# A hybrid backbone layer on one core: six fill tiles of the attention move into the Strassen stage, and TensorE's order in attention is written out as a software pipeline

## The chip, the core and the metric

The kernel runs on one core of a Trainium2 chip. A core has five engines that run side by side, each through its own list of instructions: TensorE (PE in the profile; its weight loads are the row PEld), VectorE (DVE), ScalarE (ACT), GpSimd (POOL) and SyncE (SP, which here only issues DMAs). They wait for one another through semaphores. Operands lie in the on-chip memory SBUF (128 partitions); matmul results go to PSUM, eight banks of 128 x 512 fp32 values.

The metric is the device time of the program in microseconds. Before the change it is 1123.3 us, the median of three runs (1123.12 to 1123.35).

## What is computed

One layer over 1024 latent tokens (a grid of 16 rows and 64 columns) and 256 context tokens, width 1024, fp32. The input is normalised and modulated (`h`), one wide projection feeds three branches, and the branches are merged by sigmoid gates and projected once more:

```python
h, gate = modulate(x, c, norm_g, w_ada, b_ada)
z = h @ w_in                                   # 1024 x 8704
q, k, v = per-head normalised queries and keys, values
ya = neighbourhood_attention(q, k, v, kc, vc, rpb) * silu(z[..., A_Z:B_B])
yb = bg * dw_conv(cg * val, w_conv) * silu(gz)                 # 3 taps
yc = silu(layer_norm(dw_conv(a * sigmoid(g), w31) + b)) * silu(zc)
ga, gb, gc = split(sigmoid(z[..., GATES:]), 3)
m = ga * (ya @ w_out_a) + gb * (yb @ w_out_b) + gc * (yc @ w_out_c)
x = x + gate * (m @ w_o)
```

The attention has 8 heads of 64. A query sees a clamped window of 8 rows and 16 columns with a learned bias, and all 256 context keys, in one softmax.

## The kernel before

Every fp32 operand of a large matmul is split into two rounded parts, hi and lo; a product then takes three matmuls: hi x hi, hi x lo, lo x hi (`mm3`, line 103). The 8704 columns of the wide projection are cut into tiles of 128 columns. A tile computed directly takes 2 halves of the tokens x 8 steps of depth x 3 = 48 matmuls with 512 moving columns. In the Strassen stage two tiles are computed as a pair (`group`, line 787): seven products `product` (line 770) of 4 x 3 matmuls instead of eight, with sums of the weight blocks made on POOL (`s1` to `s4`), and with sums `T` of blocks of `h` that were made earlier (`h_sums`, line 645), stored, and loaded and split again by `load_t` (line 714).

The stages, in order of time in the trace:

1. The front: modulation, the normalised `h` in its two parts (`hlf`), the queries, keys and values of the first head pair, the context, the first tile pair of the gated unit (`glu(0)`).
2. Attention. `attend(hp)` (line 586) does the four head pairs; `scores` (548) and `turned` (577) are called in 32 rounds: a round is two blocks of 128 queries of one head. In a round TensorE computes context scores `sc` and local scores `sl`; DVE adds the bias and takes the minimum (line 567); ACT makes the exponentials (568, 569); DVE sums, inverts and scales (571 to 574); TensorE transposes the probabilities (581); ACT and DVE split them into `phi` and `plo` (583, 584); TensorE multiplies them with the values (`weigh`, 598) into `py`. The score banks `sc`, `sl` and `py` exist once, the transposes' bank `pp` twice. Before a head starts, `stacks` (506) makes its split operands and `bias_of` (527) its bias image.
   The softmax chain is long, so TensorE is given fill: the queries, keys and values of the next pair (`qkv`, 130), the tiles of the gated unit (`glu`, 259), four tiles of the attention's gate path (`plain(ZA + i)`, 678), four of the short convolution's gate path (`plain(BZ + i)`, 680), and, behind the last round, two tiles of merge gates (line 725). Nobody writes down where the fill goes: the program is traced stage by stage, and a planner with a model of the engines orders each engine's list.
3. The Strassen stage: 17 groups of two tiles by `run` (952), with three steps each, then `last_two` (887) for two more pairs. Beside it DVE computes the 31-tap convolution, `conv_step(4)` and `conv_step(3)` in each group (124 steps of two instructions in all).
4. The merge of the three branches and the last projection, again by Strassen.

SBUF before: `a1` and `at` hold what attention needs and are closed behind it; `tp` (line 685) with the twelve blocks `T`, 4 KB a partition each, opens only then, so the operands of the Strassen stage are loaded behind the last round, beside the two merge gate tiles.

## Time and profile before

| | |
|---|---|
| median of three runs | 1123.3 us |
| the profiled execution | 1122.98 us, of which its span from first to last instruction is 1121.2 us |
| attention with its fill, from the first scores to the last value matmuls | 125.46 to 501.40 us |
| the two merge gate tiles behind it | 501.40 to 524.53 us |
| Strassen stage | 524.53 to about 905 us |
| merge and last projection | to 1121.2 us |
| granted TensorE clock | 0.989 of full speed on average, 1.00 in attention and in the Strassen stage |

A row of the timeline has the start and the duration in us, the engine, the line of the kernel, the operation, what it writes and reads, the shapes, and how many alike were merged; in brackets, how long the engine sat idle before it and what released it. A row of a group has line, engine, operation and shapes with its count, then the busy time in us, the mean duration in ns, and the idle time before. Matmuls overlap: the next starts before the last has ended, so the cost of one in a dense list is the distance between starts, not its duration. A row of a stretch has from and to, its length, the busy time and instructions of PE, PEld, DVE, ACT and POOL, the TensorE clock, the share of the DMA engines and GB/s.

### The profile page before, as it was taken

Reading aid. Unit: us, or ns where it says so; the run is one execution under the profiler, and the core shown is the slowest. Engines: PE = TensorE matmul, PEld = TensorE weight load, DVE = VectorE, ACT = ScalarE, POOL = GpSimd, SP = SyncE. Lnnn points to the kernel's source line nnn. Section 1 sums busy time; section 2 is a strip of 40 time slices with the busy share of each in tenths; the row PEclk is TensorE's granted clock in tenths of the full one; section 3 lists DMA queues with packets and bytes.
Section 4 is the critical chain, followed back from the end, with each engine's and each line's share of the span. In section 5 each row is a group of like instructions: output and inputs, shape, how many; then the busy total and the mean of one; then the engine's idle time right before and its main releaser. Section 6 shows DMA issues by size and latency. Waiting matters only on the chain. (4 is left out here: it accounts for less than half of the span.)

```text
span 1121.2 us, 15882 instructions
## 1 busy us (share of the span) xinstructions
PE 1084.2 (97%) x5330; PEld 923.2 (82%) x5330; DVE 832.6 (74%) x1368; ACT 519.8 (46%) x1108; POOL 653.8 (58%) x643
## 2 busy tenths in 40 slices
PE   6889999999999999999999999999999999999998
PEld 5768898998998888887888888888888788878766
DVE  6983478666765655557995997897992479879995
ACT  6764576567556554445233232323434434533430
POOL 2254957437636951104958586868777562783860
PEclk7999999999999999999999999999999999999999
DMA  9555414313312332218133424343436996462443
GB/s 351 203 190 190 122 44 120 94 57 93 118 54 85 122 120 70 67 49 326 38 132 104 151 85 160 103 153 139 129 134 237 408 327 222 140 215 66 126 155 122
DMA packets 79458, 163.17 MB, mean 146 GB/s; under 512 B 10289, under 2 KB 31153, under 8 KB 79281
## 3 DMA queue, kind: packets, MB, share of 16 engines
q1 hardware_dynamic: 74768, 160.06, 41.5%
q10 hardware_dynamic: 4608, 2.10, 0.6%
q8 instruction: 42, 0.69, 0.3%
q14 instruction: 40, 0.32, 0.1%
HBM read 120.18 MB, written 44.50 MB: 147 GB/s over the span
## 5 line engine op out<-in xcount | busy, mean ns | idle before, releaser
L751 DVE SCALAR_TENSOR_TENSOR cv<-upad,cf_t,cv 128x512 f32<-128x512 f32 x240 | 166.8, 744 | 0.1
L699 POOL TENSOR_TENSOR wl<-s,wh 128x512 fp32r<-128x512 f32 x69 | 98.4, 1439 | 21.8 <-ACT wh L698 8.1
L90 POOL TENSOR_TENSOR wl<-wr,wh 128x384 fp32r<-128x384 f32 (+1 forms) x57 | 57.3, 1012 | 68.2 <-ACT wh L88 57.6
L698 ACT CAST wh<-s 128x512 fp32r<-128x512 f32 x92 | 55.9, 616 | 87.6 <-POOL s L702 66.0
L584 DVE TENSOR_TENSOR plo<-pp,phi 128x256 fp32r<-128x256 f32 (+2 forms) x96 | 54.5, 576 | 34.8 <-ACT phi L583 34.4
L541 POOL TENSOR_TENSOR bias<-mk,img 64x96 f32<-64x96 bf16 (+1 forms) x96 | 43.7, 462 | 36.9 <-DVE mn L567 20.5
L699 POOL TENSOR_TENSOR wl<-wr,wh 128x512 fp32r<-128x512 f32 x44 | 60.5, 1375 | 4.2 <-ACT wh L698 4.2
L775 PE MATMUL ga<-ha,wh 128*128 128x512 f32 x152 | 59.3, 390 | 1.2 <-ACT wh L698 1.2
L777 PE MATMUL ga<-ha,wl 128*128 128x512 f32 x152 | 59.2, 390 | 0.0
L776 PE MATMUL ga<-ha,wh 128*128 128x512 f32 x152 | 59.2, 390 | 0.0
L583 ACT CAST phi<-pp 128x256 fp32r<-128x256 f32 (+2 forms) x96 | 46.5, 494 | 26.6 <-PE pp L581 25.9
L567 DVE CUSTOM_DVE_ANT_0 pt<-sl,bias,mn 128x384 f32<-128x384 f32 (+1 forms) x64 | 37.2, 581 | 23.0 <-PE sl L564 21.7
L88 ACT CAST wh<-wr 128x384 fp32r<-128x384 f32 (+1 forms) x66 | 31.6, 487 | 39.8 <-PE zaps L108 14.3
L568 ACT ACTIVATE pt<-sc,mn 128x256 f32<-128x256 f32 x64 | 30.4, 475 | 40.1 <-DVE mn L567 40.0
L581 PE MATMUL pp<-ident,pt 128*128 128x128 f32 x304 | 47.0, 273 | 1.6 <-DVE pt L574 1.6
L803 POOL TENSOR_TENSOR s<-wr 128x512 f32<-128x512 f32 x16 | 23.8, 1486 | 38.7 <-DMA wr<-in_wz 38.6
L581 PEld LDWEIGHTS pp<-ident,pt 128*128 128x128 f32 x304 | 37.4, 140 | 9.0 <-ACT phi L583 1.3
L79 POOL TENSOR_TENSOR ssh<-ssh,half_neg 128x4 f32<-128x4 f32 (+1 forms) x40 | 41.4, 1036 | 2.9
L574 DVE TENSOR_SCALAR pt<-pt,mn 128x640 f32<-128x640 f32 (+1 forms) x64 | 41.6, 692 | 0.9
L78 POOL TENSOR_SCALAR ssh<-ssh 128x4 f32<-128x4 f32 (+1 forms) x40 | 10.5, 261 | 53.1 <-DVE ssh L227 49.4
L964 ACT ACTIVATE c<-c 128x512 f32<-128x512 f32 x18 | 11.4, 633 | 63.6 <-DVE c L781 48.0
L109 PE MATMUL ps<-wh,hb 128*128 128x384 f32 x112 | 39.3, 354 | 1.2 <-DVE hb L353 1.1
(421 smaller groups left out, 3896.8 us busy)
## 6 DMA issues: line engine op xcount, KB each, us to landing
wr<-in_wz SPq DMA_DIRECT2D x34, 512.0 KB, 4.0
gs<-gd SPq DMA_DIRECT2D x24, 512.0 KB, 5.0
wada<-in_w_ada SPq DMA_DIRECT2D x16, 512.0 KB, 8.7
wrf<-in_wo SPq DMA_DIRECT2D x16, 512.0 KB, 3.6
wr<-in_wz SPq DMA_DIRECT2D x36, 192.0 KB, 2.4
cht<-chd SPq DMA_DIRECT2D x24, 256.0 KB, 3.1
wro<-in_wout SPq DMA_DIRECT2D x24, 256.0 KB, 5.2
gd<-gate SPq DMA_DIRECT2D x22, 256.0 KB, 4.2
```

Source lines behind the costliest of these rows:

```text
L90: lo_eng.tensor_tensor(out=lo[:, :n], in0=raw[:, :n], in1=hi[:, :n].bitcast(F32), op=ALU.subtract)
L541: pool.tensor_tensor(out=dst, in0=mv, in1=iv, op=ALU.subtract)
L574: dve.tensor_scalar(out=pt[:, SPAN - n :], in0=pt[:, SPAN - n :], scalar1=mn[:, i : i + 1], scalar2=0.5, op0=ALU.mult, op1=ALU.mult)
L581: pe.transpose(out=pp[:, c * P : c * P + P], in_=src, identity=ident)
L583: act.copy(hi, v)
L584: dve.tensor_tensor(out=lo, in0=v, in1=hi.bitcast(F32), op=ALU.subtract)
L698: act.copy(hi, src)
L699: eng.tensor_tensor(out=lo, in0=src, in1=hi.bitcast(F32), op=ALU.subtract)
L751: dve.scalar_tensor_tensor(out=acc[b], in0=src, scalar=cf_t[:, i, j : j + 1], in1=acc[b], op0=ALU.mult, op1=ALU.add)
L775: pe.matmul(ps, wh, bh, start=first and j == 0, stop=False, skip_group_check=True)
L776: pe.matmul(ps, wh, bl, start=False, stop=False, skip_group_check=True)
L777: pe.matmul(ps, wl, bh, start=False, stop=last and j == 3, skip_group_check=True)
```

## The change

- The four tiles `ZA` leave attention and become two Strassen pairs at the end of the groups; the two merge gate tiles behind attention become one pair. The stage has 20 groups and then the last two pairs; `conv_step(4)` becomes `conv_step(3)`. The factor 0.5 that undid the half-angle form of `ZA`'s SiLU leaves the scaling of the probabilities.
- In attention, TensorE's list is fixed by hand (`manual_schedule`): fill becomes generators that yield the estimated cost of each piece in us, and `pump` lets so many pieces out at two places of each round as a table of rates says (`FIRST`, `FAST`, `LAST`). A round opens the next round's context scores and first local scores, then issues all transposes of its own, a pump, the next round's second local scores, its own value matmuls, and a pump. The third transpose bank of a round is the bank `q`. The context product uses one bank instead of two.
- `stacks`, `bias_of`, `h_sums` and `load_t` become generators whose pieces are let out in the rounds (`urgent`, `later`). One operand copy of `stacks` on ACT becomes a DMA from SBUF to SBUF.
- The twelve blocks of `T` share their places (`HOMES`) with attention's operands and the front's rows; `tp` opens early. Two of the three operands `T` are loaded and split (on POOL) in the last head pair's rounds, the third behind them.

```diff
-CTX_AT = (8, 3, 3, 3)
+PUMPS = 2
+FAST = 45.9
+EARLY_ = 11
+FIRST = 13.0
+LAST = 8.0
+LOW = 300
+HOMES = ("qT", "kT", "vb", "cht0", "cht1", "qd0", "ks0", "vs0", "qlz0", "qd1", "ks1", "vs1")
...
+    def qkv_steps(hp, w, fetch):
...
+        yield from tile_mm(0)
+        yield from tile_mm(1)
+        pc = bank("psc")
+        yield from context(range(4), pc)
+        yield from tile_mm(2)
+        yield from context(range(4, KT), pc)
+        tmc, vc = context_norm(pc, state["at"] if hp % 2 else a1)
+        yield from tile_mm(3)
+        state["settle"]()
...
+    tp = ctx.enter_context(tc.tile_pool(name="tp", bufs=1, reuse_waits="tile"))
...
             act.copy(qd[hs], qT[hs])
-            act.copy(qd[os], qT[hs])
+            nc.sync.dma_start(qd[os].bitcast(F32), qd[hs].bitcast(F32))
+            yield
...
-                dve.tensor_scalar(out=pt[:, SPAN - n :], in0=pt[:, SPAN - n :], scalar1=mn[:, i : i + 1], scalar2=0.5, op0=ALU.mult, op1=ALU.mult)
...
+                dve.tensor_scalar(out=pt[:, SPAN - n :], in0=pt[:, SPAN - n :], scalar1=mn[:, q : q + 1], scalar2=None, op0=ALU.mult)
...
+            pp = ps_q.tile([P, 512], F32, tag="q", name="pp") if third else ps_p.tile([P, 512], F32, tag="pp", name="pp")
...
+        def fetch():
+            if todo:
+                ct = todo.pop(0)
+                with tc.high_priority(offset=-LOW):
+                    ready.append((ct, load_w(wz[ct], KT, pool) if ct >= 0 else qkv_weights(-ct)))
...
+        def plain_steps(ct, use):
+
+            w = weights(ct)
+            fetch()
             for b in range(2):
                 ps = ps_m.tile([P, 512], F32, tag="m", name="zaps")
-                mm3(ps, [(w[k][0], w[k][1], hcols(0, k, B512[b]), hcols(1, k, B512[b])) for k in range(KT)])
+                for k in range(KT):
+                    mm_k(ps, k, w[k][0], w[k][1], hcols(0, k, B512[b]), hcols(1, k, B512[b]))
+                    yield 0.68
+                use(b, ps)
...
+        def stream(hp):
+            if hp == 3:
+                yield from tiles(3)
+                return
+            yield from qkv_steps(hp + 1, w1 if hp == 0 else weights(-hp - 1), fetch)
+            f = tiles(hp)
...
+        def tiles(hp):
+            if hp < 2:
+                yield from glu_fill(hp + 1)
+            if hp == 2:
+                for i in (0, 1):
+                    yield from silu_fill(BZ + i, zbd[i])
+            if hp == 3:
+                yield from glu_fill(3)
+                for i in (2, 3):
+                    yield from silu_fill(BZ + i, zbd[i])
+
+        SLOTS_ = 8 * PUMPS
+        rate = [(41.0 + 21.8 - FIRST) / SLOTS_] * SLOTS_
+        rate += ([FAST / EARLY_] * EARLY_ + [(62.8 - FAST) / (SLOTS_ - EARLY_)] * (SLOTS_ - EARLY_)) * 2
+        rate += [(4 * 10.9 - LAST) / SLOTS_] * SLOTS_
...
+        def pump(hot=False):
+            clock["slot"] += 1
+            goal = FIRST + sum(rate[: clock["slot"]])
+            while clock["cost"] < goal and one():
+                pass
+            step(urgent)
+            if hot or clock["slot"] % 2 == 0:
+                step(urgent)
+            step(later)
+
         with tc.issue_after(state["kc"][0].ins), tc.issue_after(state["kc"][1].ins), tc.issue_after(state["kc"][2].ins):
-            attend(0)
-        for hp in range(4):
-            if hp:
-                attend(hp)
-            if hp < 3:
-                qkv(hp + 1, w1 if hp == 0 else None)
-            if hp < 3:
-                for j in ((), (0,), (1,))[hp]:
-                    h_sums(j)
-                glu(hp + 1)
-        for j in (2, 3):
-            h_sums(j)
-        for i in range(4):
-            plain(ZA + i, zad[i])
-        for i in range(4):
-            plain(BZ + i, zbd[i])
+            for g in (bias_of(0), stacks(0, 0)):
+                for _ in g:
+                    pass
+        with tc.manual_schedule(engines={mybir.EngineType.PE}):
+            while clock["cost"] < FIRST:
+                one()
+            ahead = open_round(0)
+            for i in range(2):
+                local(ahead, i)
+                for _ in range(5):
+                    one()
+            soften(ahead)
+            for n in range(32):
+                rd, hp, r = ahead, n // 8, n % 8
+                if r == 0:
+                    ya = at.tile([P, 16, 64], F32, tag="ya", name="ya", bufs=1)
+                    later += [bias_of(2 * hp + 1), h_sums(hp)]
+                if r == 1:
+                    urgent.append(stacks(hp, 1))
+                if r == 3:
+                    settle()
+                if r == 5 and hp < 3:
+                    later.append(bias_of(2 * hp + 2))
+                if hp == 3 and r in (2, 5):
+                    i = int(r < 5)
+                    T[i] = t_blocks(i)
+                    later.append(load_t(T[i], i, pool))
+                rd["ya"] = ya
+                if n < 31:
+                    while r == 7 and 2 * hp + 2 not in made:
+                        if urgent:
+                            settle()
+                        else:
+                            one()
+                    if r % 4 == 3:
+                        while later and len(later) > (hp == 3):
+                            step(later)
+                    ahead = open_round(n + 1)
+                    local(ahead, 0)
+                turn_local(rd, 0)
+                turn_local(rd, 1)
+                turn_context(rd)
+                pump(r > 4)
+                if n < 31:
+                    local(ahead, 1)
+                    soften(ahead)
+                weigh_round(rd)
+                pump(r > 4)
+                if r == 7:
+                    nc.sync.dma_start(yad[hp], ya.rearrange("p r c -> p (r c)"))
+            while later:
+                step(later)
+            while one():
+                pass
     a1ctx.close()
...
-    for i in (1, 0, 2):
-        load_t(T[i], i)
-    with tc.issue_after(state["py"].ins):
-        for i in (6, 7):
-            plain(GT + 2 * KT + i, gd[2 * KT + i], True)
+    T[2] = t_blocks(2)
+    for _ in load_t(T[2], 2, dve):
+        pass
...
-        conv_step(4)
+        conv_step(3)
...
-    gates = iter([KT + k for k in range(KT)] + list(range(KT)) + [2 * KT + k for k in range(KT - 2)])
+    gates = iter([KT + k for k in range(KT)] + list(range(KT)) + [2 * KT + k for k in range(KT)])
...
-    for i in range(5):
-        if i in (0, 2):
-            run(CZ + i, CZ + i + 1, zc_out(i), zc_out(i + 1))
+    for i in range(8):
+        if i % 2:
+            gate_pair()
         else:
-            gate_pair()
-        conv_step(1)
+            ct, dst = (CZ, zcd) if i < 4 else (ZA, zad)
+            i = i % 4
+            run(ct + i, ct + i + 1, silu_out(dst[i]), silu_out(dst[i + 1]))
```

485 lines of the change are left out of this document (291 added, 194 removed).

## The prediction

> **What bounds the kernel now.** I read the page first, then the busy times by stage, then TensorE's own timeline inside attention.
>
> ```profile
> span 1121.2 us, 15882 instructions
> PE 1084.2 (97%) x5330; PEld 923.2 (82%) x5330; DVE 832.6 (74%) x1368; ACT 519.8 (46%) x1108; POOL 653.8 (58%) x643
> ```
>
> TensorE is busy 97% of the span, and no other engine is over 74%. A busy share can hide slack, so I cut the span at the stage borders: attention with its fill, the last two fill tiles, the Strassen stage, the rest (columns: PE, weight load, DVE, ACT, POOL, clock, DMA).
>
> ```profile
> 125.46:501.40 375.94, 372.44 (x2149) 335.77 (x2148) 238.75 (x505) 216.18 (x564) 190.44 (x255) 1.00 0.28 88
> 501.40:524.53 23.13, 21.94 (x97) 17.83 (x95) 12.51 (x19) 11.84 (x20) 4.12 (x9) 1.00 0.91 335
> 524.53:905.00 380.47, 379.53 (x1670) 313.25 (x1671) 310.31 (x427) 139.59 (x251) 285.50 (x220) 1.00 0.44 157
> ```
>
> In attention TensorE idles 3.50 us of 375.94, before the Strassen stage another 1.19. So all three stretches end when TensorE's list ends, and what counts is the number of its instructions, the distance at which they issue, and any new wait. In the Strassen stage 1670 matmuls of 512 columns take 380.47 us: **0.228 us each** (their duration of 0.39 us overlaps). DVE (82%) and POOL (75%) have room there.
>
> **The change part by part.**
>
> *Six tiles become three pairs.* A fill tile is 2 x 8 x 3 = 48 matmuls of 512 columns (the second row: two tiles, 96 matmuls, 21.94 us). Six take 288. A Strassen pair is 7 products of 12, 84 matmuls; three take 252. TensorE loses 36 x 0.228 = **-8.2 us**. Each pair also brings POOL work (four sums, six splits) and DVE work, but in the proportion of the 19 pairs there, and the convolution's fixed 248 DVE steps are spread over 20 groups instead of 17, so DVE's share falls. I take nothing for it. The stores of the gate values move along; the first reader comes two groups and the last four tiles later.
>
> *TensorE's order.* Today the planner scatters the transposes of the probabilities. A run of them costs something behind it:
>
> ```profile
> 300.45 0.60 PE L581 MATMUL pp<-ident,pt 128*128 128x128 f32 x4
> 300.81 0.42 PE L108 MATMUL ps<-wl,ha 128*128 128x384 f32 x1
> 301.07 0.34 PE L109 MATMUL ps<-wh,ha 128*128 128x384 f32 x1
> 301.24 0.34 PE L107 MATMUL ps<-wh,ha 128*128 128x384 f32 x1
> ```
>
> The first matmul after the run holds the place for 0.26 us, the next for 0.17: 0.09 us per run.
>
> ```profile
> L581 PE MATMUL pp<-ident,pt 128*128 128x128 f32 x304 | 47.0, 273 | 1.6 <-DVE pt L574 1.6
> L583 ACT CAST phi<-pp 128x256 fp32r<-128x256 f32 (+2 forms) x96 | 46.5, 494 | 26.6 <-PE pp L581 25.9
> ...
> 138.46 0.33 PE L581 MATMUL pp<-ident,pt 128*128 128x128 f32 x1 [0.43 <-DVE pt L574]
> 498.09 0.38 PE L581 MATMUL pp<-ident,pt 128*128 128x128 f32 x2
> ```
>
> Three evictions in each of 32 rounds make 96; the timeline shows 83 separate runs, from 138.46 to 498.09. The new order issues a round's nine or ten transposes in a row: 32 runs. 51 x 0.09 = **-4.6 us** (bounds 0 and -5.8, if all 96 were apart).
>
> *Waits that exist.* The 3.50 + 1.19 us above can go or stay: **-4.7 us** at most. I take them off and put in the new waits whole.
>
> *Waits that come.* In the new order a round's first transpose stands at a fixed place, and everything behind it on TensorE, fill included, waits with it. It needs the chain score matmul, DVE sum and minimum, two exponentials, sum, reciprocal, scaling. Undisturbed, in the last round:
>
> ```profile
> 493.23 0.28 PE L564 MATMUL sl<-ks,qlz 128*128 128x256 f32 x1
> 493.65 0.48 DVE L567 CUSTOM_DVE_ANT_0 pt<-sl,bias,mn 128x256 f32<-128x256 f32 x1 [0.40 <-PE sl L564]
> 494.18 0.47 ACT L568 ACTIVATE pt<-sc,mn 128x256 f32<-128x256 f32 x1 [1.74 <-DVE mn L567]
> 494.64 0.50 ACT L569 ACTIVATE pt<-pt,mn 128x256 f32<-128x256 f32 x1
> 495.66 0.95 DVE L574 TENSOR_SCALAR pt<-pt,mn 128x640 f32<-128x640 f32 x2
> ```
>
> 2.43 us to the scaling, half of 0.95 more for the first one: 2.9 us, some 3.2 where the tile is 384 wide. What lies in front of the transposes is the value matmuls (0.3 us in the first round of a half, 1.9 in the second), one pump of fill, and the next scores (0.8). A pump is, by the list's own sums (they agree with 0.228 us a matmul), 3.1 us in the first head pair, 4.2 then 3.4 in the next two, and 2.2 in the last, where only four tiles are left for 16 pumps. So in the last pair an even round has 0.3 + 2.2 + 0.8 = 3.3 us of cover for a chain of 3.2: I take 0.3 us for four rounds, 1.2. In the other pairs cover is 4.2 to 5.4 us in the short rounds, 5.8 to 7.0 in the long ones. But the chain is not always quick:
>
> ```profile
> 130.92 0.34 PE L564 MATMUL sl<-ks,qlz 128*128 128x384 f32 x1
> 137.91 0.95 DVE L574 TENSOR_SCALAR pt<-pt,mn 128x512 f32<-128x512 f32 x2
> ...
> 390.76 0.28 PE L564 MATMUL sl<-ks,qlz 128*128 128x256 f32 x1
> 397.33 0.55 DVE L574 TENSOR_SCALAR pt<-pt,mn 128x640 f32<-128x640 f32 x1
> ```
>
> The first round takes 6.99 us, a late one 6.57, behind operand copies and weight splits on ACT and DVE. Read so in all 32 rounds, from this first to the last above, 16 stay within 3.2 us and six exceed 6. Those six had no haste, since TensorE had other work; I let half of the excess remain, about 3.5 us. At the start only ten fill pieces lie between the first scores and the first transposes, and the exponential's table load stands in it:
>
> ```profile
> 127.56 1.28 ACT L568 ACT_TABLE_LOAD   x1 [2.10 <-DVE mn L567]
> ```
>
> I take 1.5 us. At the end 8 us of fill, not 21.9, cover the way into the Strassen stage. Today's wait there is not for want of cover but for the place of the weights:
>
> ```profile
> 523.38 0.60 ACT L640 ACTIVATE flt<-zaps 128x512 f32<-128x512 f32 x1 [4.84 <-PE zaps L109]
> 523.87 0.61 ACT L698 CAST wh<-wry 128x512 fp32r<-128x512 f32 x1
> 524.53 0.50 PE L775 MATMUL ga<-ha,wh 128*128 128x512 f32 x1 [1.19 <-ACT wh L698]
> ```
>
> The split follows the last fill tile at once; the same happens after. Two of the three Strassen operands are by then loaded inside attention, and the third has two products' time. I take 1.9 us (bounds 1.2 and 5, if the raw weights' DMA comes late). Sum of new waits: 1.2 + 3.5 + 1.5 + 1.9 = **+8.1 us**, bounds 3 and 24.
>
> *Edits at nothing.* A DMA replaces eight operand copies:
>
> ```profile
> L517 ACT CAST qd<-qT x8: 1045/1047/1052, 113.1 to 392.5; 64x1024 fp32r<-64x1024 f32 x8
> cht<-chd SPq DMA_DIRECT2D x24, 256.0 KB, 3.1
> ```
>
> 1.05 us of ACT goes, and the nearest load of that size lands after 3.1 us, 2 us later; the copies are started rounds ahead, which hides it. Without that cover, 2 us at each of three pair borders. Without the tiles' activations DVE's work in attention falls from 238.75 us to about 233 and ACT's from 216.18 to about 202; over the shorter stage that is 70% and 61% instead of 64% and 58%. SP carries the same transfers, eight operand loads among them earlier by up to 60 us.
>
> Sum against the profiled execution's 1122.98 us (span 1121.2; median of the runs 1123.3): 1122.98 - 8.2 - 4.6 - 4.7 + 8.1 = **1113.6 us**.
>
> **The rivals.**
>
> *Nearly dense.* The fast chains are the rule, ACT and DVE are busy 58% and 64% of attention, and new waits come to 3 us: 1108.5.
>
> *The lock of POOL.* The scaling shows two prices:
>
> ```profile
> 381.31 2.56 DVE L574 TENSOR_SCALAR pt<-pt,mn 128x640 f32<-128x640 f32 x2
> 381.98 1.54 POOL L649 TENSOR_TENSOR hsum<-hb 128x512 f32<-128x512 f32 x1
> 405.69:484.33 78.64, 78.64 (x406) 67.15 (x405) 41.55 (x88) 37.05 (x102) 17.41 (x20) 1.00 0.22 76
> L699 POOL TENSOR_TENSOR wl<-wr,wh 128x512 fp32r<-128x512 f32 x44 | 60.5, 1375 | 4.2 <-ACT wh L698 4.2
> L90 POOL TENSOR_TENSOR wl<-wr,wh 128x384 fp32r<-128x384 f32 (+1 forms) x57 | 57.3, 1012 | 68.2 <-ACT wh L88 57.6
> L541 POOL TENSOR_TENSOR bias<-mk,img 64x96 f32<-64x96 bf16 (+1 forms) x96 | 43.7, 462 | 36.9 <-DVE mn L567 20.5
> ```
>
> Two scalings take 0.95 us beside an idle POOL and 2.56 beside a working one. Through most of the last pair POOL is busy 22% now (17.41 of 78.64). After, it does there eight operand splits (1.4 us each), eight sums (1.4), twelve weight splits (1.0) and twelve bias pieces (0.46): 40 us in some 61, 66%, just where cover is thinnest. A scaling then meets a POOL instruction two times in three and waits half of 1.4: 0.47 us, for 16 scalings 7.5, half of it hidden in the long rounds: +3.8, 1117.4. The Trainium skill, "SBUF — State Buffer", section "SBUF: two separate sides", has the reason and speaks against this move: the port pair that DVE and GpSimd share is "an exclusive lock, not a bandwidth split". The trace agrees, with its 2.56 us.
>
> *The front.* The context's keys are turned before the first scores. Now two fill tiles lie between the last context matmul and that turn:
>
> ```profile
> 109.28 0.34 PE L107 MATMUL ps<-wh,ha 128*128 128x384 f32 x1
> 117.45 0.29 DVE L229 TENSOR_TENSOR tmc<-rawc,ssh 128x128 f32<-128x128 f32 x1 [0.88 <-POOL ssh L79]
> ```
>
> If the handwritten order keeps fill behind the turn, TensorE waits those 8.2 us: 1121.8. Against it: only the order within the list is fixed, and the list opens with just these tiles.
>
> *Slower: ordered starvation.* If every short round of the first three pairs runs its chain in 390.76's 6.57 us, cover of 4.2 to 5.4 falls short by 2.4 in four rounds and by 1.2 to 2 in eight: 21 us. With 1.2 + 1.5 + 1.9 the waits are 25.6, and the time 1131.1. It decides from (8.2 + 4.6 + 4.7 - 4.6) / 1.8, seven such rounds. For it: six of 32 chains are that long today. Against it: today's planner could afford them.
>
> **How the numbers follow.** Forecast 0.42, nearly dense 0.17, POOL's lock 0.15, the front 0.10, slower 0.16. The most likely time is **1113.6**. The range leaves out most of the slower case and the lower edge of the dense one: **1106.5 to 1125**. A difference of 0.2%, 2.25 us, is about what a measurement of this kernel can tell from no change. The front case lies just around that border, and so do edges of the others: **faster 0.75, same 0.08, slower 0.17**.
>
> **What would show it.** The Strassen stage must hold 252 matmuls more at 0.228 us, 57 us. Attention with its fill must shrink from 399 us to about 332. Runs of transposes must number near 32, and TensorE's idle time in attention must be near 8 us, its rows naming the scaling. A first transpose of a round late by over 0.5 us on average refutes the waits; a wait of 5 us or more near 110 us shows the front; scalings of over 1 us in the last pair show the lock.

## The result, and the profile after

The changed kernel takes 1153.05 us (median of four runs, 1152.55 to 1154.83) where the kernel before took 1123.24 (1123.12 to 1123.35, four runs beside them): a ratio of 1.0268, 95% interval 1.0251 to 1.0286. It is 29.8 us slower; 1113.6 was predicted, and the range ended at 1125.

The head of the page, and the same cut into stages (attention to the last value matmul, the way to the first Strassen product, the Strassen stage, the rest; columns as before):

```profile
span 1150.7 us, 15879 instructions
PE 1089.8 (95%) x5294; PEld 926.1 (80%) x5294; DVE 844.6 (73%) x1378; ACT 518.1 (45%) x1106; POOL 685.7 (60%) x663
```

```profile
0.00:132.66 132.66, 108.28 (x544) 93.34 (x545) 92.64 (x175) 78.13 (x151) 64.92 (x92) 0.91 0.63 220
132.66:476.40 343.74, 327.52 (x1912) 298.22 (x1912) 226.18 (x498) 204.37 (x542) 171.19 (x238) 0.98 0.29 86
476.40:487.60 11.20, 9.95 (x45) 7.89 (x44) 2.95 (x5) 2.90 (x5) 2.57 (x6) 1.00 0.92 309
487.60:916.70 429.10, 422.68 (x1848) 347.50 (x1849) 328.96 (x446) 151.15 (x272) 311.25 (x239) 1.00 0.41 142
```

TensorE has its 36 matmuls less (5330 to 5294), and yet every stretch has more than its matmuls need. To see where, I split the distances between TensorE's starts in four. *Dense* is the count times the distance at which matmuls of a width issue in a full list (0.227 us at 512 columns, 0.174 at 384, 0.119 at 256, 0.092 at 128). *Idle* is what the rows have in brackets. *Slow* is the excess where matmuls follow at about double the dense distance. The rest is runs of transposes and steps in between. The Strassen stage is taken to its last product here, 888.18 us before the change and 916.72 after; the 905 us that stood for its end ahead of the prediction take in 17 us of the merge.

| us | before | after | difference |
|---|---|---|---|
| front, to the first scores | 125.5 | 132.7 | +7.2 |
| attention and the way to the first product | 399.1 | 355.0 | -44.1 |
| of it dense | 380.8 | 316.6 | -64.2 |
| of it idle | 4.6 | 17.0 | +12.4 |
| of it slow | 3.3 | 9.5 | +6.2 |
| of it the rest | 10.4 | 11.9 | +1.5 |
| Strassen stage | 363.6 | 429.1 | +65.5 |
| of it dense | 362.0 | 419.1 | +57.1 |
| merge and last projection, to the last matmul | 229.1 | 230.1 | +1.0 |

So the count came true, -64.2 + 57.1 = -7.1 us. Against it stand 7.2 us in the front, 20.1 in attention, 8.4 in the Strassen stage and 1.0 behind it: 36.7 us. The slow time is not all the clock: before, the granted clock is 1.00 through the whole of attention, so those 3.3 us are something else. After, about 6.2 of the 9.5 us lie in stretches at half clock.

TensorE's waits from the first scores to the first product, and in the Strassen stage (what waited, on what; us in total, times, the longest):

```profile
PE pp L646 <- DVE pt L690: 13.5, 11, 4.1
PE sc L660 <- ACT pt L685: 1.3, 1, 1.3
PE ga L1009 <- ACT wh L317: 1.3, 1, 1.3
...
PE gd L1009 <- DVE c L1015: 5.2, 4, 2.4
```

The first row is the first transposes of a round waiting for the scaled probabilities. Most of it is two rounds. This is the timeline of the first of them, at the border of two head pairs, on ACT, DVE and POOL, then TensorE:

```profile
205.80 1.05 ACT L604 CAST qd<-qT 64x1024 fp32r<-64x1024 f32 x1
206.75 1.04 ACT L612 CAST ks<-kT 64x1024 fp32r<-64x1024 f32 x1
207.82 0.47 ACT L685 ACTIVATE pt<-sc,mn 128x256 f32<-128x256 f32 x1
...
206.88 1.85 DVE L607 TENSOR_TENSOR qlz<-qT,qd 64x1024 fp32r<-64x1024 f32 x1 [0.62 <-ACT qd L604]
208.76 1.37 DVE L614 TENSOR_TENSOR ks<-kT,ks 64x1024 fp32r<-64x1024 f32 x1
210.17 0.31 DVE L687 TENSOR_TENSOR mn<-mn 128x2 f32<-128x2 f32 x1
...
211.63 2.05 DVE L690 TENSOR_SCALAR pt<-pt,mn 128x640 f32<-128x640 f32 x2
...
207.59 3.89 POOL L635 TENSOR_TENSOR bias<-mk,img 64x144 f32<-64x144 bf16 x4
211.56 1.27 POOL L794 TENSOR_TENSOR hsum<-hsum 128x512 f32<-128x512 f32 x1
```

```profile
213.32 1.35 PE L646 MATMUL pp<-ident,pt 128*128 128x128 f32 x9 [3.67 <-DVE pt L690]
214.43 0.62 PE L118 MATMUL zaps<-ha,wh 128*128 128x512 f32 x1
214.85 0.63 PE L119 MATMUL zaps<-ha,wh 128*128 128x512 f32 x1
...
218.62 0.39 PE L120 MATMUL zaps<-hb,wl 128*128 128x512 f32 x1
218.84 0.39 PE L118 MATMUL zaps<-hb,wh 128*128 128x512 f32 x1
```

Operand copies of the next pair stand ahead of the second block's two exponentials on ACT and of the round's sum on DVE. They are for that pair's second head, whose first scores come at 259 us: the places that they write have just come free, but nobody waits for them. The copies on DVE take 1.85 and 1.37 us, against 1.22 elsewhere, while POOL works on the bias, and the two scalings take 2.05 us, where they took 0.95 in the last round before, while POOL works on a sum of `h`. TensorE's list is fixed, so the fill behind the transposes waits too. And this wait is paid for again: for 3.4 us behind it the 512-wide matmuls start 0.42 us apart instead of 0.23.

The front has a picture of its own, on POOL, DVE and TensorE:

```profile
114.05 2.28 POOL L789 TENSOR_TENSOR hsum<-hb 128x512 f32<-128x512 f32 x1
...
119.72 1.28 POOL L789 TENSOR_TENSOR hsum<-ha 128x512 f32<-128x512 f32 x1
120.96 2.53 POOL L794 TENSOR_TENSOR hsum<-hsum 128x512 f32<-128x512 f32 x2
123.45 1.01 POOL L96 TENSOR_TENSOR wl<-wr,wh 128x384 fp32r<-128x384 f32 x1
124.55 1.32 POOL L84 TENSOR_SCALAR ssh<-ssh 128x2 f32<-128x2 f32 x2
```

```profile
116.60 0.29 DVE L290 TENSOR_REDUCE ssh<-tmc 128x2 f32<-128x128 f32 x1 [0.20 <-ACT tmc L288]
...
119.07 6.48 DVE L614 TENSOR_TENSOR ks<-kT,ks 64x1024 fp32r<-64x1024 f32 x1
```

```profile
127.45 0.33 PE L200 MATMUL pskc<-ident,tmc 128*128 128x128 f32 x1 [2.43 <-DVE tmc L292]
...
129.46 0.53 PE L120 MATMUL ps<-wh,ha 128*128 128x384 f32 x1
129.78 0.53 PE L118 MATMUL ps<-wh,ha 128*128 128x384 f32 x1
```

The sums of the context keys' squares are ready by 116.9 us, but POOL takes them up at 124.55: two memsets, sums of `h`, which nobody needs yet, and a weight split come first. The change itself brings the sums here: it puts `h_sums(0)` on the list of side work with the first round, where the kernel before called it with the second head pair's fill (its first sum runs at 178.5 us, the changed kernel's at 94.5). A DVE copy beside them takes 6.48 us instead of its usual 1.22. The key turn waits, and behind it the 384-wide matmuls start 0.32 us apart instead of 0.17.

### The profile page after: what moved, and what is told of

Same layout as the page of the kernel before. It is cut to its first block, busy times and chain, and to the rows that moved or that the text cites. A ratio compares the mean times of both kernels' runs of the same rounds, so it can differ in the third digit from the quotient of the medians.

```text
span 1150.7 us, 15879 instructions
## 1 busy us (share of the span) xinstructions
PE 1089.8 (95%) x5294; PEld 926.1 (80%) x5294; DVE 844.6 (73%) x1378; ACT 518.1 (45%) x1106; POOL 685.7 (60%) x663
## 5 line engine op out<-in xcount | busy, mean ns | idle before, releaser
L318 POOL TENSOR_TENSOR wl<-s,wh 128x512 fp32r<-128x512 f32 x78 | 111.5, 1441 | 24.8 <-ACT wh L317 16.8
L317 ACT CAST wh<-s 128x512 fp32r<-128x512 f32 x104 | 63.6, 616 | 99.9 <-POOL s L950 81.9
L318 POOL TENSOR_TENSOR wl<-wr,wh 128x512 fp32r<-128x512 f32 x53 | 73.9, 1395 | 4.5 <-ACT wh L317 4.5
L1009 PE MATMUL ga<-ha,wh 128*128 128x512 f32 x176 | 68.7, 390 | 1.7 <-ACT wh L317 1.3
L1011 PE MATMUL ga<-ha,wl 128*128 128x512 f32 x176 | 68.6, 390 | 0.6 <-POOL wl L318 0.6
L1010 PE MATMUL ga<-ha,wh 128*128 128x512 f32 x176 | 68.5, 389 | 0.0
L1037 POOL TENSOR_TENSOR s<-wr 128x512 f32<-128x512 f32 x19 | 28.5, 1498 | 64.3 <-DMA wr<-in_wz 57.5
L635 POOL TENSOR_TENSOR bias<-mk,img 64x96 f32<-64x96 bf16 (+1 forms) x96 | 44.1, 465 | 19.9 <-DVE mn L677 12.9
L646 PE MATMUL pp<-ident,pt 128*128 128x128 f32 x304 | 42.5, 284 | 13.6 <-DVE pt L690 13.5
L96 POOL TENSOR_TENSOR wl<-wr,wh 128x384 fp32r<-128x384 f32 (+1 forms) x39 | 39.2, 1016 | 23.9 <-ACT wh L94 15.4
L317 ACT CAST wh<-wr 128x512 fp32r<-128x512 f32 x60 | 37.0, 617 | 14.3 <-DMA wr<-in_wz 10.5
L1009 PEld LDWEIGHTS ga<-ha,wh 128*128 128x128 f32 x176 | 33.0, 188 | 9.3 <-ACT wh L317 1.7
```

Of the source, the lines that this page charges most:

```text
L317: act.copy(hi, src)
L318: eng.tensor_tensor(out=lo, in0=src, in1=hi.bitcast(F32), op=ALU.subtract)
L635: pool.tensor_tensor(out=dst, in0=mv, in1=iv, op=ALU.subtract)
L646: pe.transpose(out=pp[:, c * P : c * P + P], in_=src, identity=ident)
L1009: pe.matmul(ps, wh, bh, start=first and j == 0, stop=False, skip_group_check=True)
L1010: pe.matmul(ps, wh, bl, start=False, stop=False, skip_group_check=True)
```

## The experiments

Two theories stood at the start. *Order*: TensorE's fixed list makes the waits, and the planner's order would take them away. *Cover*: with six tiles fewer, attention no longer has the matmuls to hide its softmax chain behind, in either order. What the first runs showed brought three more: copies, GpSimd, and the place of the fill. Each row's ratio is against the kernel before on the same chip; idle and slow are of attention to the last value matmul, from one profiled execution of each kernel.

| run | median us | ratio (95% interval) | first scores at | attention idle + slow | to the first product | Strassen stage |
|---|---|---|---|---|---|---|
| before | 1123.24 | | 125.5 | 3.4 + 3.1 | 23.4 | 363.6 |
| after | 1153.05 | 1.0268 (1.0251 to 1.0286) | 132.7 | 15.7 + 9.3 | 11.2 | 429.1 |
| x1 planner's order | 1145.82 | 1.0206 (1.0161 to 1.0251) | 135.0 | 10.3 + 7.3 | 7.7 | 427.0 |
| x4 only the tiles | 1153.34 | 1.0273 (1.0230 to 1.0316) | 124.2 | 11.9 + 9.0 | 15.5 | 427.4 |
| x6 all but the tiles | 1143.03 | 1.0173 (1.0117 to 1.0229) | 132.3 | 10.1 + 9.3 | 28.8 | 365.5 |
| x7 two pairs, planner | 1129.25 | 1.0063 (1.0043 to 1.0083) | 124.2 | 9.5 + 6.4 | 23.4 | 400.9 |
| x8 one pair, planner | 1128.12 | 1.0051 (1.0037 to 1.0064) | 125.5 | 7.6 + 6.5 | 23.4 | 381.1 |
| x11 x8, fill held back | 1125.69 | 1.0029 (1.0018 to 1.0040) | 126.1 | 5.8 + 4.5 | 23.4 | 381.1 |
| x16 x8, matmuls held back | 1128.97 | 1.0053 (1.0039 to 1.0067) | 126.8 | 8.7 + 5.4 | 23.4 | 381.1 |
| x12 x7, fill held back | 1133.68 | 1.0099 (1.0085 to 1.0113) | 123.9 | 14.8 + 7.5 | 23.4 | 401.0 |
| x2 early fill | 1154.27 | 1.0281 (1.0232 to 1.0331) | 133.4 | 16.6 + 10.1 | 11.2 | 429.0 |
| x3 side work apart | 1152.64 | 1.0267 (1.0221 to 1.0312) | 132.6 | 15.7 + 10.8 | 11.2 | 429.8 |
| x9 copies' priority | 1153.16 | 1.0272 (1.0255 to 1.0289) | 132.6 | 15.4 + 9.9 | 11.2 | 429.7 |
| x10 late key turn | 1159.57 | 1.0331 (1.0313 to 1.0349) | 138.3 | 16.9 + 8.5 | 11.2 | 429.7 |
| x13 hold behind DVE | 1154.87 | 1.0288 (1.0274 to 1.0302) | 132.7 | 15.5 + 11.0 | 11.2 | 429.7 |
| x14 border | 1161.75 | 1.0349 (1.0333 to 1.0365) | 132.7 | 22.0 + 13.9 | 11.2 | 430.1 |
| x17 hold behind POOL | 1151.90 | 1.0265 (1.0246 to 1.0285) | 127.7 | 18.9 + 10.3 | 11.2 | 429.2 |
| x18 without the sums | 1136.92 | 1.0134 (1.0112 to 1.0155) | 122.5 | 12.7 + 5.3 | 11.1 | 430.6 |
| x5 conv_step(4) | 1147.34 | 1.0211 (1.0172 to 1.0251) | 132.6 | 15.3 + 9.3 | 11.2 | 424.6 |
| x15 x13, x14, x5 | 1155.25 | 1.0293 (1.0274 to 1.0313) | 132.8 | 20.2 + 12.7 | 11.2 | 423.5 |

x3, x9 and x13 turned out to run the changed kernel's own lists: every instruction of TensorE, DVE, ACT and POOL comes in the same order as without their edits. They test none of their theories, but they show the scatter: ratios of 1.0267 to 1.0288, 25.3 to 26.5 us of idle and slow time against the changed kernel's 25.1, and 429.7 or 429.8 us in the Strassen stage against 429.1. x1, x4, x10, x11, x12, x14, x15 and x16 came out at times that neither side of their forecasts had named.

### Order or cover: x1, x4, x6

x1 is the changed kernel with TensorE's list given back to the planner:

```diff
-        with tc.manual_schedule(engines={mybir.EngineType.PE}):
+        with ExitStack():
```

> The changed kernel, but the planner orders TensorE's list in attention too; the pieces and the rate table stay. Theory 'fixed order' (a late scaling stops everything behind it, because nothing else may go ahead): the waits on the scaling and the slow clock behind them go, attention shrinks by 15 us or more, 1135 us or less. Rival 'crowding' (ACT, DVE and POOL have too much to do in the shorter stage, so the scaling is late in any order): the waits only change places, 1147 to 1157 us.

x4 is the kernel before with nothing but the six tiles moved, in the planner's order:

```diff
-        for i in range(4):
-            plain(ZA + i, zad[i])
...
-    with tc.issue_after(state["py"].ins):
-        for i in (6, 7):
-            plain(GT + 2 * KT + i, gd[2 * KT + i], True)
...
-        conv_step(4)
+        conv_step(3)
...
+            ct, dst = (CZ, zcd) if i < 4 else (ZA, zad)
```

> The kernel before with only the six tiles moved into three Strassen pairs; the planner orders all lists as before, and the operands of the Strassen stage are loaded behind attention, now without the two gate tiles beside them. Theory 'fixed order': the tiles alone give the 8.2 us of the count, less what the uncovered loads cost (12 loads and splits, 8 to 14 us): 1115 to 1129. Rival 'crowding': with six tiles less, attention starves under the planner too, by 10 us or more beyond that: 1130 to 1145. Third, 'Strassen is dear' (its added groups wait for DVE as in the changed kernel, 8 us): the stage's waits show it.

x6 is the changed kernel with all six tiles back in attention, in the written-out order:

```diff
-todo = [CGL + 1, CA + 1, -2, ...
+todo = [CGL + 1, CA + 1, ZA, -2, ..., ZA + 2, ZA + 3, GT + 2 * KT + 6, GT + 2 * KT + 7]
...
+                yield from silu_fill(ZA + hp, zad[hp])
...
+                for i in (6, 7):
+                    yield from gate_fill(2 * KT + i)
...
-FAST = 45.9
+FAST = 51.0
```

> TensorE's order in attention written out as in the changed kernel, but all six tiles computed in attention again (pumps of 3.8 to 4.6 us, 4.1 in the last head pair, the two gate tiles behind the last round), 19 pairs in the Strassen stage. This fills the fourth field beside before (planner, tiles in attention: 6.5 us of waits and slow clock there), the changed kernel (fixed, moved: 25) and x4_six (planner, moved: 21). Theory 'cover' (fill is what hides the softmax chain, in either order): waits and slow clock in attention fall to 8 to 12 us; with the front's 7 us more, 1128 to 1136 us. Rival 'fixed order': they stay at 20 or more, 1140 to 1150.

Take idle and slow time of attention and of the way to the first product together: 7.9 us before, 22.8 with everything but the moved tiles (x6), 36.2 with the tiles alone (x4), 26.5 with both. Either half of the change alone adds 14.9 us or more, so neither theory holds alone. x6 holds more than the order: the side work in pieces, the shared places and the copy by DMA are in it too. Of x4's sum 15.1 us is one wait:

```profile
474.41 0.40 PE L600 MATMUL py<-plo,vc 128*128 128x512 f32 x1
489.92 0.80 PE L770 MATMUL ga<-ha,wh 128*128 128x512 f32 x1 [15.11 <-ACT wh L696]
```

Nothing is left to compute while the operands `T` are loaded and split. That wait the change does avoid, by loading two of the three in the last pair's rounds: its first product waits 1.25 us. But without it x4 has 21 us as well, where the kernel before has 6.5. And the planner's order does the changed kernel some good in attention (x1, 17.6 instead of 25.1 us), but the first product then waits 7.1 us instead of 1.25. x1's ratio is 0.6% lower, and the intervals just touch.

x6 and x1 also begin attention late, like the changed kernel, and x4 does not: the front's loss belongs neither to the tiles nor to the fixed order.

### How many tiles, and where: x7, x8, x11, x12, x16

x7 is x4 with the merge gates left as cover and `conv_step(4)` kept; x8 moves one pair only, `ZA + 2` and `ZA + 3` (its values are doubled before they are stored, since the factor 0.5 stays):

```diff
-        for i in range(4):
+        for i in range(2):
             plain(ZA + i, zad[i])
...
+            run(ZA + 2, ZA + 3, silu_out(zad[2], True), silu_out(zad[3], True))
```

> The kernel before with only the four tiles of the attention's gate path moved, as two pairs; the two gate tiles stay behind attention and cover the loads; four convolution steps as before. Theory 'cover': the count gives 5.5 us, attention's waits and slow clock rise from 6.5 by two thirds of what x4_six showed (10 us): 1126 to 1132, and the Strassen stage shows under 2 us of waits. Rival 'only the loads were bare' (x4_six lost its 15.1 us in front of the first product and little else): 1116 to 1121.

> As x7_four with only two tiles moved, as one pair. Theory 'cover', if the loss grows faster than the number of tiles: the count's 2.7 us are kept in part, 1120 to 1123. If the loss is in proportion: 1124 to 1128.

A pair saves 12 matmuls, 2.7 us. x8 is 5.8 us slower instead (1128.12 against 1122.28 for the kernel before on the same chip), with 7.6 us more idle and slow time in attention. The stages of x7, three rows, and the last rounds of x8, one, show where it arises:

```profile
124.20:420.00 295.80, 293.71 (x1742) 269.32 (x1741) 194.37 (x413) 180.71 (x469) 179.22 (x241) 1.00 0.30 95
420.00:436.00 16.00, 16.00 (x87) 13.78 (x86) 9.36 (x20) 5.50 (x16) 0.74 (x1) 1.00 0.09 34
436.00:468.60 32.60, 25.07 (x130) 19.04 (x129) 25.24 (x65) 20.51 (x61) 0.00 (x0) 0.90 0.02 9
...
464.00:488.50 24.50, 19.45 (x92) 16.22 (x91) 17.50 (x42) 13.43 (x39) 0.20 (x6) 0.79 0.03 11
```

Up to 436 us x7's TensorE is busy but for 2.1 us. Then the fill is used up, and the last rounds run bare: 7.5 us idle in 32.6, with POOL silent. In x8 it is 5.05 us in the last 24.5. So the planner spends the fill early, and what is missing is missing in the last rounds. x11 holds two of x8's tiles back:

```diff
+                if i in {2: 3, 3: 5}:
+                    held.enter_context(tc.issue_after(sent_at[24 + {2: 3, 3: 5}[i]].ins))
                 plain(BZ + i, zbd[i])
```

> The kernel before with one pair moved (1128.1 us), and two of its fill tiles held back to the second half of the last head pair. Theory 'the fill runs out before the rounds do': the fill is the same and only its place is changed; the waits of 1 to 2 us at 466 to 484 us go, idle and slow time in attention fall from 14.1 us to 9 or less, and the time is 1121 to 1124 us, level with the kernel before or up to 0.2% better. Rival 'each moved tile leaves its wait wherever the rest stands': the waits appear earlier in the last pair, idle and slow time stay at 12 to 15 us, 1126 to 1130 us.

> The kernel before with two pairs (the four ZA tiles) moved (1129.3 us), and three of the four fill tiles left for the last head pair held back to its second, fourth and sixth round. Theory 'the fill runs out before the rounds do': the stretch without fill from 436 to 468 us goes, idle and slow time in attention fall from 15.9 us to 11 or less, 1122 to 1126 us. Rival 'too little fill in all': four tiles cannot cover eight rounds, each round waits a little, idle and slow time stay at 14 to 18 us, 1127 to 1132 us.

> The kernel before with one pair moved; the weights of all fill tiles are loaded early, and only the matmuls of three of the last head pair's six tiles are held back, to its second, fourth and fifth round. In x11 the waits (2.3 us of idle time between 435 and 450 us) stood where the next tile's weights were not yet split. Theory 'place of the fill': these go, idle and slow time in attention fall from 10.2 us to 7.5 or less, 1120.5 to 1123.5 us against 1122.7 to 1123.3 of the kernel before. Rival 'amount of the fill': 1124.5 to 1128 us.

x12 holds three of x7's four tiles in the same manner, and x16 only the matmuls of three of x8's tiles, with their weights loaded early. Holding fill back brings x8 0.2% (the intervals just touch): idle and slow time fall from 14.1 to 10.2 us, not to the 9 of the theory, and x11 stays 0.3% slower than the kernel before. In x12 idle and slow time grow to 22.3 us, and x16 gives back what x11 had gained. So with one pair the place of the fill is part of the price, though a second way of holding it back (x16) brought nothing; with two pairs the one place that was tried made it worse. No run beats the kernel before.

### The written-out order's details: x2, x3, x9, x10, x14

x2 counts the rate table from the fill already spent, so that the first pumps are not empty. x3 lets POOL's side work wait while operand copies are let out. x9 gives the copies a lower priority:

```diff
-            goal = FIRST + sum(rate[: clock["slot"]])
+            goal = clock["base"] + sum(rate[: clock["slot"]])
```

```diff
-            step(later)
+            if not urgent:
+                step(later)
```

```diff
+                with tc.high_priority(offset=-100 if queue is urgent else 0):
+                    done = next(queue[0], 1)
```

> The changed kernel, with the ten fill pieces that it lets out between the first scores counted, and the first head pair's remaining fill spread evenly over its 16 pumps, so that the first pumps are not empty. Theory 'empty pumps': the waits near 142 to 148 us (0.22 + 1.34 + 1.95, and 2.7 us of half clock behind them) go, 1147 us. Rival 'crowding': the first rounds wait for the same chain, only with fill pieces between, under 1 us gained.

> The changed kernel, but no bias image, block sum or operand load is let out by a pump while operand copies of the next head are still under way. Theory 'collision' (the two waits of 3.67 and 4.05 us come because POOL's side work holds DVE's copies and scalings in the same rounds): both fall under 1.5 us and the half clock behind them goes, 6 to 10 us, 1143 to 1147. Rival 'copies alone' (ACT and DVE copies in front of the exponentials make the chain late): both waits stay within 1 us, 1151 to 1154.

> The changed kernel, but the pieces that make the next head's operands (stacks) are let out at a lower priority, so that exponentials and scalings of the running round go first on ScalarE and VectorE. Theory 'copies ahead of the softmax': the two longest waits of TensorE in attention, 3.67 us at 213 and 4.05 us at 310, both behind such copies, fall under 1.5 us each, idle and slow time in attention fall from 25.1 us to 18 or less, and the time is 1144 to 1148 us. Rival 'the rounds are short of fill wherever the copies stand': the waits move to other rounds, or to the first scores of the next head, whose operands come late; 1151 to 1156 us.

None changes the time by more than 0.15%. In x2 the waits near 142 to 148 us go, and 0.70 and 1.92 us at the next turn of context keys (149.55 and 151.77 us) come, so empty pumps are not what costs the time. x3 and x9 left every engine's list as it was, so neither collision nor the copies' place is tested by them. Why the lower priority moved nothing was not followed up.

x10 turns the first context keys in the middle of the opening fill. x14 is to hold the copies behind the scalings and, at the border of two pairs, puts a round's transposes, a pump and its values ahead of the next pair's scores:

```diff
-        context_turn(tmc, q_bank("pskc"), kcT)
+        state["turn"] = lambda: context_turn(tmc, q_bank("pskc"), kcT)
...
+            while clock["cost"] < FIRST / 2:
+                one()
+            state["turn"]()
```

```diff
+                if border:
+                    while 2 * hp + 2 not in made:
+                        if urgent:
+                            with tc.issue_after(rd["scaled"].ins):
+                                settle()
+                        else:
+                            one()
+                    weigh_round(rd)
+                    ahead = open_round(n + 1)
```

> The changed kernel, but the context keys of the first head pair are turned in the middle of the opening fill instead of in front of it. Theory 'the front waits for the key turn': the waits of 2.43 and 0.46 us at the turn go, and with them the half clock behind them (384-wide matmuls at 0.32 instead of 0.17 us for some 3 us), so the first scores come 4 to 6 us earlier and the time is 1147 to 1149.5 us. Rival 'the wait moves': the first scores then wait for the operands made from the turned keys, and the time is 1151 to 1155 us.

> The changed kernel, but operand copies are let out only behind a round's scaling, and at the border of two head pairs a round's transposes, a pump of fill and its value matmuls come before the next pair's first scores. Theory 'the copies stand ahead of the last round's softmax': the waits at 213, 310 and 403 us (3.67, 4.05, 1.18 us) and the half clock behind them go, idle and slow time in attention fall from 25.1 us to 16 or less, 1142 to 1147 us. Rival 'the border has no cover': the first scores of the next pair, or their first transposes, wait instead for operands made later, and idle and slow time stay at 22 us or more, 1150 to 1157 us.

Both came out slower than either side expected. In x10 the turn waits longer, and the reason is not TensorE's list:

```profile
120.28 6.39 DVE L614 TENSOR_TENSOR ks<-kT,ks 64x1024 fp32r<-64x1024 f32 x1
...
128.66 0.45 PE L200 MATMUL pskc<-ident,tmc 128*128 128x128 f32 x1 [6.91 <-DVE tmc L292]
```

The keys are no earlier, so TensorE only stands still at another place. x14 did half of what it was to do: on DVE the copies at the first border come some 39 us later (245.9 us), on ACT theirs still run ahead of the second block's exponentials (205.82 and 206.78 us, the exponential at 207.84). The waits of 3.67 and 4.05 us go, and others come:

```profile
PE sl L673 <- DVE mn L677: 11.6, 7, 3.4
PE pp L646 <- DVE pt L690: 8.7, 9, 1.9
```

The local scores of the next rounds now wait for their bank, which DVE reads late. Neither side had named that.

### GpSimd: x13, x17, x18

x13 holds POOL's side work behind the scaling, and was to test the front and the borders at once. x17 holds that of the first pair behind the context keys' powers:

```diff
+            with tc.issue_after(rd["scaled"].ins):
+                step(later)
```

```diff
+        kc0 = state["kc"][0]
...
+                behind = kc0 if hp == 0 else None
...
+                    held.enter_context(tc.issue_after(behind.ins))
+                step(later)
```

> The changed kernel, but GpSimd's side work of attention (bias pieces, sums of h, operand splits) is let out only behind the scaling of the running round. Theory 'GpSimd in the way': in the front the sums of h no longer stand ahead of the context keys' square root, the operand copy that takes 6.48 us takes 1.2 to 2.2 us, and the first scores come 4 to 7 us earlier; at 213 and 310 us scaling and copies run undisturbed and the two waits fall from 7.7 us together to 4 or less. Time 1142 to 1148 us. Rival 'GpSimd is incidental': the front gains under 2 us, the waits stay, 1150 to 1156 us.

> The changed kernel, but GpSimd's side work of the first head pair (sums of h, bias of the second head) is queued behind the context keys' powers on GpSimd. In the changed kernel two sums, four more steps and a weight split stand ahead of those powers, from 114 to 124.6 us. Theory 'GpSimd's queue holds up the key turn': the powers come 3 to 7 us earlier, the wait of 2.43 us at the turn and the half clock behind it go, the first scores come 4 to 7 us earlier than 132.7 us; the time is 1146 to 1149.5 us. Rival 'something else is late next in the front' (the queries' operands, the last weights): first scores at 131 us or later, 1151 to 1155 us.

In these runs the hold moved only instructions of the engine that it names. x13 names one of DVE, so POOL's order stayed (the sum is still at 114 us), and it tests nothing. x17 names one of POOL, and the front does what the theory says: the powers' first step runs at 120.3 instead of 124.6 us, the waits at the turn fall from 2.9 to 0.4 us, the first scores come 5.0 us earlier. But idle and slow time in attention grow by 4.1 us, more than the scatter of 1.4, the first of it at once: where scores waited 1.34 us for an exponential of the first round, they now wait 3.40. The ratio stays within the changed kernel's interval. The rival's time came, though not for its reason.

x18 takes the sums of `h` off POOL; it leaves out arithmetic that the layer needs:

```diff
-                t = tmp("hsum")
-                pool.tensor_tensor(out=t, in0=hlf[o][k][:, 0].bitcast(F32), in1=hlf[o][k][:, 1].bitcast(F32), op=ALU.add)
-                return t
+                return hlf[o][k][:, 0].bitcast(F32)
...
-                pool.tensor_tensor(out=b, in0=a, in1=b, op=ALU.subtract)
```

> The changed kernel without the arithmetic of the sums of h: the high parts of h are stored in their place, with the same transfers, so that 32 instructions of 1.3 us leave GpSimd and the Strassen operands T hold other numbers. Theory 'GpSimd's work stretches copies and scalings in attention': idle and slow time in attention fall from 25.1 us to 19 or less, beside what the front gains. Rival 'short of cover in any case': attention stays at 23 us or more, and the gain is the front's alone (4 to 7 us, 1146 to 1149 us).

```profile
122.50:460.90 338.40, 325.11 (x1913) 296.27 (x1912) 220.41 (x498) 204.10 (x543) 138.54 (x217) 0.98 0.26 79
```

16 us go (15 by the ratios), of them 10.2 in the front and 5.3 in attention, where idle and slow time fall from 25.1 to 18.0, as the theory said; the waits at the first two borders of head pairs fall from 3.67 and 4.05 us to 2.15 and 1.18. POOL is off TensorE's path by its own shares (171 busy of 344 us, now 139 of 338), and still its sums are the largest single cause that these runs could take away. The kernel before does the same sums, but none ahead of the powers, as said above, and with all the fill in attention.

### The Strassen stage: x5, x15

```diff
-        conv_step(3)
+        conv_step(4)
```

> The changed kernel with four convolution steps instead of three in the middle of each Strassen group, as before the change. In every kernel with the six tiles moved so far, the stage has waited 3.4 to 7.2 us for DVE's sums, with 1.5 to 3.4 us of slow clock behind them, against 0.8 before. Theory 'rhythm' (the thinner convolution leaves the planner's list of DVE with the sums behind longer instructions): the stage falls from 429 to some 421 us, 1145 us. Rival 'load' (DVE has too much beside the pairs): it stays at 428 to 431.

> Both edits together, and conv_step(4). If all three add up (front 5, attention 9, Strassen stage 4.5 us): 1133 to 1138 us. If only the convolution's part holds: 1146 to 1150 us.

x5 makes the stage 4.5 us shorter. Of the waits for DVE's `c` is left:

```profile
PE gd L1009 <- DVE c L1015: 2.3, 2, 2.1
```

Of the 8.4 us the step size is thus about half. x15 keeps that part (423.5 us). Its ratio is what x14's loss and x5's gain make together (1.0268 + 0.0081 - 0.0057 = 1.0292, measured 1.0293), since x13's edit changes nothing; the gains that were forecast for the front and for attention are not there.

## Why the prediction was wrong

The profiled execution took 1152.55 us, 39 us more than the forecast, and no single term carries that: idle time 8.9, the clock 6.2, the transposes 6.1, the front 7.2, the Strassen stage 8.4, and some 2 in the count and the merge. The step that failed in the sum is *Waits that come*, sized too low; the clock behind such waits, the front and the Strassen stage stood in the sum at nothing.

- **Count, -8.2: right.** 36 matmuls less in the list; dense time fell by 7.1 us. The Strassen stage got the 57 us that were named.
- **Transposes, -4.6: did not come, though the runs did.** They stand in 32 runs where 83 were, and the rest, which holds what runs cost, still went from 10.4 to 11.9 us. The rows were misread:

```profile
161.09 1.25 PE L646 MATMUL pp<-ident,pt 128*128 128x128 f32 x10
162.10 0.42 PE L118 MATMUL ps<-wh,hb 128*128 128x384 f32 x1
162.35 0.33 PE L119 MATMUL ps<-wl,hb 128*128 128x384 f32 x1
```

  Ten transposes hold 1.01 us, and the matmul behind them 0.08 more than its 0.17: 0.11 us a transpose. The run of four that the prediction shows holds 0.36 us and 0.09 behind it: 0.11 a transpose too. The step behind a run is thus no price of the run; fewer, longer runs had nothing to save.
- **Waits that exist, -4.7:** they went, and are lost in what came.
- **Waits that come, +8.1: this is the step that failed.** Idle time alone became 17.0 us. By its parts: the last pair 1.4 (predicted 1.2), the way to the first product 1.25 (1.9), the start 3.5 (1.5), and the slow chains 3.67 + 4.05 + 1.18 + 0.73 = 9.6 (3.5). I let half of the slow chains' excess remain because they had had no haste. On the whole the chains did get quicker: read as before, 20 of the 32 stay within 3.2 us and two exceed 6, where it was 16 and six. But the last rounds of the first three head pairs stayed long (6.18, 7.47 and 5.37 us to the scaling). The first two had only 4.2 and 4.9 us of cover, and their first scalings alone took 1.6 and 1.3 us, against 0.5. In these rounds the lists of ACT and DVE, which the planner still ordered, put the operand copies of a head that is not yet due ahead of the round's softmax, and POOL works beside them, as the rows from 205.80 us on show.
- **No term at all: the clock.** Behind three waits (1.95, 3.67 and 4.05 us) TensorE runs at half the rate: 6.2 us more in attention. The wait of 3.67 us is followed by nine matmuls in 3.72 us (214.43 to 218.15) that take 2.04 in a full list, and so costs 5.3.
- **Strassen stage, nothing: 8.4.** DVE's share fell as argued, from 83% (301.63 of 363.65 us in the kernel before) to 77% (328.96 of 429.1). A share did not say when `c` is ready.
- **The rival "the front"** had the right place, the context key turn, and a wrong reason: not TensorE's list but POOL's queue, as x10 and x17 show. It came in addition to the rest. x17 gave 5.0 of its 7.2 us back, and the time did not follow.
- **The rival "POOL's lock"** was priced for the scalings of the last pair only, with POOL busy 66% there. POOL is busy 37% (27.04 of 72.90 us from 403.50 on), two of the 16 scalings take over 1 us, where four did before, and TensorE's longest wait for one is 0.89 us. What is seen is slow copies and scalings beside a working POOL at the borders and a slow copy in the front; with POOL's queue, this costs 15 to 16 us (x18 takes out both together).
- **The rival "ordered starvation"** had the sign. Its mechanism, many short rounds late by a little, is not what the trace shows: eleven waits, of which the two longest make 7.7 of 13.5 us. That is 0.42 us a round on average. The sign named for the waits, over 0.5 us on average, thus did not show: an average hides two long waits.

Open: 18 us of idle and slow time remain without the sums, against 6.5 before. x4 and x6 show that fewer tiles cost this much without the new order, and the new structure without fewer tiles; what in that structure does it with all the fill in place was not separated. No run moved the copies at the borders without moving something else, so that they and POOL's work make the long waits is read from the trace and borne out by x18 for POOL's part only. The places that `T` shares with attention's operands, the copy turned into a DMA and the single context bank were not undone.

## What to carry to other kernels

Matmuls that hide a softmax chain have a value besides their count: take them away only if the chain has slack in every round, the last ones above all, where a planner that spends early has left nothing. When one engine's order is written out by hand, look at the order of the engines that feed it, for each of their delays now stops everything behind it; that writing theirs out too would pay is not shown here (x14 tried it in part and lost). An engine that is busy half the time can set the pace, so follow the releaser of a wait back to the queue it stood in before judging by shares. And before an edit is believed to test a theory, compare the engines' lists with and without it: three edits here moved nothing.

## What the hardware showed

- The granted clock changes only at the borders of steps of 3.41 us, and the half rate goes with how much of a step TensorE was idle, not with the length of one wait. These stretches, cut at the steps, stand around the waits of 1.34 and 1.95 us and of 3.67 us:

```profile
142.92:146.33 3.41, 1.27 (x7) 0.77 (x6) 2.44 (x8) 2.58 (x10) 3.10 (x6) 1.00 0.27 77
146.33:153.16 6.83, 5.67 (x21) 5.41 (x22) 4.04 (x11) 2.71 (x7) 4.31 (x11) 0.50 0.00 0
...
211.19:214.60 3.41, 1.28 (x10) 1.11 (x11) 2.67 (x5) 1.78 (x6) 3.12 (x6) 1.00 0.20 77
214.60:218.01 3.41, 3.41 (x10) 2.63 (x9) 1.98 (x4) 0.63 (x2) 3.08 (x5) 0.50 0.36 106
```

  In both, a step with 2.1 us idle is followed by half clock. In the twenty traces of this case, between 115 and 1060 us, all 50 full-clock steps with 1.95 us or more of idle time are followed by a step at half clock, and none with under 0.95 is; in between, either happens. So the wait of 1.95 us at 147.49 costs more because 1.34 us came just before it: the 384-wide matmuls behind it start 0.32 us apart. After 1.18 us at 403.49 the 512-wide ones start 0.23 apart from the second on.

```profile
147.49 2.52 PE L646 MATMUL pp<-ident,pt 128*128 128x128 f32 x10 [1.95 <-DVE pt L690]
...
150.13 0.52 PE L119 MATMUL ps<-wl,ha 128*128 128x384 f32 x1
150.45 0.52 PE L120 MATMUL ps<-wh,ha 128*128 128x384 f32 x1
...
403.49 1.35 PE L646 MATMUL pp<-ident,pt 128*128 128x128 f32 x9 [1.18 <-DVE pt L690]
...
404.91 0.39 PE L119 MATMUL zaps<-ha,wh 128*128 128x512 f32 x1
405.14 0.40 PE L120 MATMUL zaps<-ha,wl 128*128 128x512 f32 x1
```

  The Trainium skill, "TensorE: Matmul & The Clock Gate", part 1, lets the half rate come after an idle window of about 3.4 us. The step length agrees; here 2.1 us idle within one was enough.

- A DVE instruction beside POOL can take five times as long. The copy of 119.07 us takes 6.48 us, across four POOL instructions in a row (119.72 to 124.46) and into the next, and 1.22 us undisturbed. The Trainium skill, "SBUF — State Buffer", section "SBUF: two separate sides", describes the shared port pair as locked for one instruction at a time; that agrees with a delay, and the trace shows that it need not end with the first of them.
